# Fixing TensorE's order in the chunk recurrence of a hybrid RWKV-7 / RG-LRU block

## The chip, the cores and the metric

The kernel runs on one core of a Trainium2 chip. The metric is the device time of one execution in microseconds (us), less is better. Times of the kernel before come from three runs; the profile comes from one more execution.

## The reference, cut to what matters

One block over 512 frames of width 1024: a token mixer of two branches, then cross-attention into a memory of 256 rows, then a gated ConvFFN. The change lies in the token mixer, where one input projection of 4864 columns feeds all of it:

```python
h = rms_norm(x, norm_mix_g[l])
proj = h @ w_in[l] + b_in[l]
y_a = rwkv7_branch(proj[..., :cb0], ...) @ w_branch_a[l]
y_b = rglru_branch(proj[..., cb0:cb1], proj[..., cb1:cb2], ...) @ w_branch_b[l]
merged = sigmoid(proj[..., cb2:cg1]) * y_a + sigmoid(proj[..., cg1:]) * y_b
x = x + merged @ w_mix_out[l]
```

The first branch is a recurrence over time for 8 heads of 64:

```python
sa = einsum('bhij,bhj->bhi', state, a_t)
state = state * w_t[:, :, None, :] + sa[..., None] * b_t[:, :, None, :] + v_t[..., None] * k_t[:, :, None, :]
y_t = einsum('bhij,bhj->bhi', state, r_t)
```

The second is a convolution of width 4, two gates and a linear scan (`a = exp(log_a)`, `h_t = a_t h_{t-1} + u_t`), times `gelu(py)`.

## The kernel before

All activations lie with channels on the 128 partitions and the 512 frames along the free axis. A projection of 128 output columns (a "block") accumulates 8 steps over 1024 input rows. Each step is three TensorE products of 128x512, because every operand is split in a high and a low part (`mm3`, lines 159 to 163: high x high, high x low, low x high; lines 160 to 162 of the trace). Weights stream in units of 128x1024: SyncE loads them, ScalarE casts the high part (`win_h`), VectorE subtracts it from the original (`win_l`, line 115). The input projection has 38 blocks. Blocks 0 to 13 feed the RWKV branch, blocks 14 to 17 the convolution and the gates of the RG-LRU branch (`px_gates`), 18 to 21 its gelu (`py_block`), 22 to 37 the merge gates (`gate_block`). `IN_REST` lists the last 24 of them in the order of issue: 22 to 37, then 14 to 21. The first three are issued early.

The recurrence is worked in 8 chunks of 64 frames, with all heads at once. One chunk (`chunk`) is a chain of small TensorE groups, with the steps of other engines between them:

- `x`: the state and the chunk's values against the keys (`UV`, `AK`); VectorE copies it to `Xs`.
- `y`, first half: what the state adds to the output.
- `u`: `Xs` through the inverted chunk matrix; ScalarE copies one half to `UV`, VectorE the other.
- `vr`: the next chunk's values turned round (`rows_v`); VectorE takes their mean (`vm`) and subtracts it into the next `UV`.
- `s`: the new state; VectorE scales it (`Sn`) and writes it into the next `UV`, and prepares `SP`.
- `y`, second half; ScalarE copies it to `yT`.
- `kbr`: the next chunk's keys turned round (`rows_kb`), two halves; ScalarE copies them to `KBr`.

The accumulator banks are shared: `vr` and `kbr_0` use one (tag "kv"), `s` and `kbr_1` another ("s"), `x` and `u` a third ("xu"), `y` a fourth. A group that takes over a bank waits until the last reader of it is done.

What sets the order: the whole recurrence is emitted first, under a very high priority, and the rest of the input projection after it in the program. A scheduler then builds one fixed list for each engine. It takes by priority what it estimates to be ready, so projection products fall between the small groups wherever it thinks that one has to wait. On VectorE a part of the recurrence's steps is kept in program order (`pin`). Each engine works through its list in order on the chip, and an instruction whose operand isn't ready holds up all that stand behind it.

The RG-LRU part of the same stretch: for each of four branches `b`, `px_gates` evacuates the block (ScalarE's Identity), adds three shifted terms on VectorE (line 802), multiplies the two gate matrices (`ga`, `gx`, lines 806 and 808) on TensorE, and after each pair `px_scan` runs table functions on ScalarE and a scan into `YB` on VectorE (line 824). The tile `xb` has two buffers, so branch 2 takes over that of branch 0. `group_norm` normalizes `y`, half by half. The products `yb_ps` of the second branch follow.

At the other end of the kernel the ConvFFN's hidden blocks come in pairs (`fx_ps`, `fyz_ps`); the last pair is blocks 20 and 21. VectorE then forms their activation (`fs`, `fa`, `graw`) and the low parts of the late blocks (`gl`, `gr`). The output products `fo_ps` need `wfo_h` and `wfo_l` of the output weights and the split blocks `g`.

Of the kernel before, what the change touches and what calls it, by code (L numbers as in the profile page):

```python
# [32 lines left out]
NEARLY = 3  # L33
IN_ORDER = IN_RWKV + IN_REST
# [19 lines left out]
def hybrid_block_kernel(ctx: ExitStack, tc: tile.TileContext, xT_d, mT_d, pv_d, cst_d, win_d, wk_d, wv_d,  # L54
# [95 lines left out]
    def sum_exact(ps, blocks, src, pool, tag, name, **kw):  # L150

        hi = pool.tile(list(src.shape), F32R, tag=tag, name=f"{name}_h", **kw)
        lo = pool.tile(list(src.shape), F32R, tag=tag, name=f"{name}_l", **kw)
        S.copy(hi, src)
        V.tensor_tensor(lo, src, hi.bitcast(F32), ALU.subtract)
        PE.matmul(ps, blocks, hi, start=True, stop=False)
        PE.matmul(ps, blocks, lo, start=False, stop=True)

    def mm3(ps, lh, ll, rh, rl, start, stop, **kw):
        first = PE.matmul(ps, lh, rh, start=start, stop=False, **kw)  # L160
        PE.matmul(ps, lh, rl, start=False, stop=False, **kw)  # L161
        PE.matmul(ps, ll, rh, start=False, stop=stop, **kw)  # L162
        return first
# [407 lines left out]
    def gate_block(b):  # L571
        ps = inproj(22 + b)
# [4 lines left out]
    for jp in range(2):  # L577
# [10 lines left out]
        for j in js:  # L588
            if j == 3:
                for i in IN_REST[:NEARLY]:  # L590
                    gate_block(i - 22)
# [76 lines left out]
    pin = tc.keep_in_program_order  # L668
# [4 lines left out]
    def rows_v(c):  # L673
# [3 lines left out]
        for e in range(2):  # L677
            hs, oh = half[e], half[1 - e]
            for j in range(NPAIR):
                o = ps[oh, j * HD:(j + 1) * HD]  # L680
                src = vT[hs, j, c * HD:(c + 1) * HD]
                if e:
                    PE.transpose(o, src, ident[hs, hs])
                else:
                    PE.matmul(o, src, ident[hs, hs], start=True, stop=True)
# [8 lines left out]
    def rows_kb(c):  # L694
        KBr = ch.tile([P, 2, NPAIR, HD], F32, tag="KBr", name=f"KBr{c}", bufs=2)
        for e in range(2):
            ps = ch_ps(f"kbr{c}_{e}", ("kv", "s")[e])
            for j in range(NPAIR):
                PE.transpose(ps[:, j * HD:(j + 1) * HD], kb_cols(j, e, c), ident[half[e], half[e]])
# [6 lines left out]
    def chunk(c, UV, KBr, SP):  # L706
# [3 lines left out]
        for j in range(NPAIR):  # L710
            for e in range(2):
                PE.matmul(psx[half[e], j * HD:(j + 1) * HD], AK[:, e, j * NC + c, 0:HD], UV[:, e, j, :],
                          start=True, stop=True)
# [3 lines left out]
        for j in range(NPAIR):  # L717
            for e in range(2):
                PE.matmul(psy[half[e], j * HD:(j + 1) * HD], UV[:, e, j, :], AK[:, e, j * NC + c, HD:P],
                          start=(j == 0), stop=False)  # L720
        psu = ch_ps(f"u{c}", "xu")
        for j in range(NPAIR):
            for e in range(2):
                hs = half[e]
                PE.matmul(psu[hs, j * HD:(j + 1) * HD], BZ[hs, j * NC + c, 0:HD], Xs[hs, j, :],
                          start=True, stop=True)
        S.copy(UV[half[0], 0], j3(psu[half[0], 0:256]))
        pin(V.tensor_copy(UV[half[1], 1], j3(psu[half[1], 0:256])))
        if not last:
            nUV = rows_v(c + 1)  # L730
            pss = ch_ps(f"s{c}", "s")
            for j in range(NPAIR):
                for e in range(2):
                    PE.matmul(pss[half[e], j * HD:(j + 1) * HD], KBr[:, e, j, :], UV[:, e, j, :],
                              start=True, stop=True)
        for j in range(NPAIR):
            for e in range(2):
                hs = half[e]
                PE.matmul(psy[hs, j * HD:(j + 1) * HD], UV[hs, e, j, :], BZ[hs, j * NC + c, HD:P],
                          start=False, stop=(j == NPAIR - 1))  # L740
# [24 lines left out]
    ya2 = pa.tile([P, 2, 4, T], F32R, tag="AR", name="ya2")  # L765


    def group_norm(hf, jp, ps, psg):
# [9 lines left out]
        sum_exact(ps, bonesr, y2.rearrange("p j t -> p (j t)"), tp, "xb", f"gv{nm}", bufs=2)  # L778
# [18 lines left out]
    def px_gates(b):  # L797
        ps = inproj(14 + b)
# [6 lines left out]
        psa = rw_ps(f"ga{b}", prg, tag="rg")  # L805
        PE.matmul(psa, rg[:, 0, b, :], xb, start=True, stop=True)
        psx = rw_ps(f"gx{b}", prg, tag="rg")
        PE.matmul(psx, rg[:, 1, b, :], xb, start=True, stop=True)
        ga = tp.tile([P, T], F32, tag="ga", name=f"ga{b}", bufs=2)
        gx = tp.tile([P, T], F32, tag="gx", name=f"gx{b}", bufs=2)  # L810
        tab(ga, psa, AF.Sigmoid, bias=par("b_ga", b))
# [449 lines left out]
```

## Time and profile before

| what | value |
|---|---|
| median of 3 runs | 936.24 us (935.5 to 937.24) |
| profiled execution | 938.62 us, its span 936.8 us |
| granted TensorE clock, mean | 0.997 |
| TensorE busy | 917.8 us of the span |
| VectorE busy | 638.1 us |
| ScalarE busy | 468.9 us |
| DMA, mean rate | 183 GB/s |
| input projection products (line 160 of the trace) | 304, 404 ns mean |

Times in the trace run from the start of the span. A TensorE duration covers the pipelined flight of a product, so successive products overlap; what a product costs is read from start to start. The trace writes two records for a product of plain float32 operands, and one for the split ones and for transposes. A group's row gives line, engine, operation, output and inputs, shape, count, busy time and mean; behind the second bar stands idle time before it and what ended it. In a timeline, brackets show an idle time and its releaser.

### The profile page before, as it was taken

Reading aid. Unit: us, or ns where it says so; the run is one execution under the profiler, and the core shown is the slowest. Engines: PE = TensorE matmul, PEld = TensorE weight load, DVE = VectorE, ACT = ScalarE, POOL = GpSimd, SP = SyncE. Lnnn points to the kernel's source line nnn. Section 1 sums busy time; section 2 is a strip of 40 time slices with the busy share of each in tenths; the row PEclk is TensorE's granted clock in tenths of the full one; section 3 lists DMA queues with packets and bytes.
Section 4 is the critical chain, followed back from the end, with each engine's and each line's share of the span. In section 5 each row is a group of like instructions: output and inputs, shape, how many; then the busy total and the mean of one; then the engine's idle time right before and its main releaser. Section 6 shows DMA issues by size and latency. Waiting matters only on the chain.

```text
span 936.8 us, 14783 instructions
## 1 busy us (share of the span) xinstructions
PE 917.8 (98%) x5856; PEld 770.8 (82%) x5856; DVE 638.1 (68%) x1043; ACT 468.9 (50%) x711; POOL 87.9 (9%) x101
## 2 busy tenths in 40 slices
PE   6999999999999999999999999999999999999996
PEld 6778777788877667777887777999999999888886
DVE  7774688668845767775575578788888778833333
ACT  6565665522335276334454466766556556532221
POOL 0102211000022200001111111111111000000000
PEclk9999999999999999999999999999999999999998
DMA  8778787364599922758886668799999755422202
GB/s 273 262 255 238 174 220 190 122 170 143 158 225 194 192 35 77 218 181 221 216 226 158 167 136 195 220 264 266 259 273 252 228 188 187 140 90 90 92 22 91
DMA packets 87813, 171.16 MB, mean 183 GB/s; under 512 B 23552, under 2 KB 28800, under 8 KB 87744
## 3 DMA queue, kind: packets, MB, share of 16 engines
q1 hardware_dynamic: 61728, 111.10, 36.9%
q0 software_dynamic: 18688, 47.19, 25.0%
q10 hardware_dynamic: 7328, 11.92, 3.8%
q8 instruction: 46, 0.75, 0.3%
q14 instruction: 23, 0.19, 0.1%
HBM read 158.92 MB, written 57.41 MB: 231 GB/s over the span
## 4 chain that ended last, share of the span: by engine, by line
PE 95%; DMA 2%; ACT 1%; DVE 1%; issue 0%; POOL 0%; DVEq 0%; SPq 0%; ACTq 0%
PE in_ps L162 8%; PE in_ps L161 8%; PE in_ps L160 8%; PE fx_ps L160 4%; PE fx_ps L162 4%; PE fx_ps L161 4%; PE fo_ps L161 4%; PE fo_ps L160 4%; PE fo_ps L162 4%; PE fyz_ps L160 3%; PE fyz_ps L162 3%; PE fyz_ps L161 3%; PE co_ps L160 2%; PE mix_ps L160 2%; PE q_ps L161 2%; PE mix_ps L161 2%
## 5 line engine op out<-in xcount | busy, mean ns | idle before, releaser
L161 PE MATMUL in_ps<-hT,win_h 128*128 128x512 f32 x304 | 123.6, 407 | 0.0
L162 PE MATMUL in_ps<-hT,win_l 128*128 128x512 f32 x304 | 122.8, 405 | 0.0
L126 ACT CAST wfi_h<-wfi_r 128x1024 fp32r<-128x1024 f32 x77 | 81.0, 1052 | 83.4 <-PE fx_ps L161 28.2
L160 PE MATMUL in_ps<-hT,win_h 128*128 128x512 f32 x304 | 122.2, 404 | 0.0
L127 DVE TENSOR_TENSOR wfi_l<-wfi_r,wfi_h 128x1024 fp32r<-128x1024 f32 x77 | 94.2, 1223 | 39.0 <-ACT wfi_h L126 38.6
L420 POOL DMA_DIRECT2D dS<-in_wfi x66 | 66.6, 1036 | 458.5 <-PE in_ps L160 152.3
L114 ACT CAST win_h<-win_r 128x1024 fp32r<-128x1024 f32 x38 | 39.9, 1050 | 87.7 <-PE in_ps L161 79.2
L115 DVE TENSOR_TENSOR win_l<-win_r,win_h 128x1024 fp32r<-128x1024 f32 x38 | 46.4, 1222 | 50.2 <-ACT win_h L114 50.1
L161 PEld LDWEIGHTS in_ps<-hT,win_h 128*128 128x128 f32 x304 | 57.0, 188 | 15.7 <-issue 1.9
L160 PEld LDWEIGHTS in_ps<-hT,win_h 128*128 128x128 f32 x304 | 57.0, 188 | 15.3 <-issue 1.4
L162 PEld LDWEIGHTS in_ps<-hT,win_l 128*128 128x128 f32 x304 | 57.0, 187 | 15.1 <-issue 1.7
L115 DVE TENSOR_TENSOR wfo_l<-wfo_r,wfo_h 128x1024 fp32r<-128x1024 f32 x22 | 26.9, 1224 | 52.1 <-ACT wfo_h L114 52.1
L114 ACT CAST wfo_h<-wfo_r 128x1024 fp32r<-128x1024 f32 x22 | 23.1, 1048 | 62.1 <-PE fo_ps L161 61.4
L160 PE MATMUL fx_ps<-hq,wfi_h 128*128 128x256 f32 x176 | 50.1, 285 | 1.2 <-ACT wfi_h L126 0.9
L162 PE MATMUL fx_ps<-hr,wfi_l 128*128 128x256 f32 x176 | 49.7, 283 | 0.0
L160 PE MATMUL fx_ps<-hr,wfi_h 128*128 128x256 f32 x176 | 49.7, 282 | 0.0
L160 PE MATMUL fyz_ps<-hq,wfi_h 128*128 128x256 f32 x176 | 49.4, 281 | 0.0
L161 PE MATMUL fx_ps<-hr,wfi_h 128*128 128x256 f32 x176 | 49.4, 280 | 0.0
L161 PE MATMUL fx_ps<-hq,wfi_h 128*128 128x256 f32 x176 | 49.3, 280 | 0.0
L161 PE MATMUL fyz_ps<-hq,wfi_h 128*128 128x256 f32 x176 | 49.2, 280 | 0.0
L162 PE MATMUL fx_ps<-hq,wfi_l 128*128 128x256 f32 x176 | 49.0, 278 | 0.0
L162 PE MATMUL fyz_ps<-hq,wfi_l 128*128 128x256 f32 x176 | 49.0, 278 | 0.0
(421 smaller groups left out, 2514.2 us busy)
## 6 DMA issues: line engine op xcount, KB each, us to landing
dS<-in_wfi POOLq DMA_DIRECT2D x66, 512.0 KB, 8.3
wfi_r<-dS SPq DMA_DIRECT2D x44, 512.0 KB, 6.0
win_r<-in_win SPq DMA_DIRECT2D x38, 512.0 KB, 4.2
wfi_r<-in_wfi SPq DMA_DIRECT2D x33, 512.0 KB, 5.8
dS<-dS POOLq DMA_DIRECT2D x22, 512.0 KB, 5.5
wfo_r<-in_wfo SPq DMA_DIRECT2D x22, 512.0 KB, 3.4
wv_r<-in_wv SPq DMA_DIRECT2D x8, 512.0 KB, 5.9
dG<-gs ACTq DMA_DIRECT2D x16, 256.0 KB, 2.1
```

Source lines behind the costliest of these rows:

```text
L114: S.copy(hi[:, o:o + n], raw[:, o:o + n])
L115: V.tensor_tensor(lo[:, o:o + n], raw[:, o:o + n], hi[:, o:o + n].bitcast(F32), ALU.subtract)
L126: S.copy(hi, raw)
L127: V.tensor_tensor(lo, raw, hi.bitcast(F32), ALU.subtract)
L160: first = PE.matmul(ps, lh, rh, start=start, stop=False, **kw)
L161: PE.matmul(ps, lh, rl, start=False, stop=False, **kw)
L162: PE.matmul(ps, ll, rh, start=False, stop=stop, **kw)
L420: return lambda: nc.gpsimd.dma_start(s(out), src, **kw)
```

## The change

The order of TensorE's work through the 8 chunks is written out instead of left to the scheduler. `chunk` becomes a generator that stops after the first half of `y` and again at its end. The rest of the input projection becomes a generator too (`rest`), one step (three products) at a time. `fill(n)` takes n of its steps. 16 blocks (128 steps) come ahead of the recurrence; then each chunk gets 1 step at its first stop and 4 at its second, the last chunk only the first; what is left comes after. While `pinned` is set, `mpin` puts every product of recurrence, projection and gates in program order on TensorE. The gate products are no longer issued right after their convolution but one at a time, at every fourth step of the following blocks (`next_gate`). The first half's group norm starts ahead of blocks 20 and 21 and goes on after five steps of them. `pin` no longer fixes VectorE's program order as a whole, it chains the recurrence's steps on VectorE among themselves.

```diff
+NMID = 16
     def sum_exact(ps, blocks, src, pool, tag, name, **kw):
...
         V.tensor_tensor(lo, src, hi.bitcast(F32), ALU.subtract)
+        yield
         PE.matmul(ps, blocks, hi, start=True, stop=False)
...
+    pinned = [False]
+    def mpin(ins):
+        return tc.keep_in_program_order(ins) if pinned[0] else ins
     def mm3(ps, lh, ll, rh, rl, start, stop, **kw):
-        first = PE.matmul(ps, lh, rh, start=start, stop=False, **kw)
+        first = mpin(PE.matmul(ps, lh, rh, start=start, stop=False, **kw))
...
-    pin = tc.keep_in_program_order
+    behind = []
+    def pin(ins):
+        if behind:
+            tc.add_manual_dep(ins.ins, behind[-1].ins.name, mybir.DependencyInfo(
+                mybir.DependencyClass.NoSync, mybir.DependencyReason.DATA), reason="order of the recurrence")
+        behind.append(ins)
+        return ins
...
+        yield 1
         psu = ch_ps(f"u{c}", "xu")
...
         S.copy(yT[:, :, c * HD:(c + 1) * HD], j3(psy[:, 0:256]))
+        if not last:
+            yield 4
         return nUV, nKB, SP
...
-    with tc.high_priority(offset=1000000):
-        UV, KBr, SP = rows_v(0), rows_kb(0), None
-        for e in range(2):
-            V.memset(UV[half[e], e], 0.0)
-        for c in range(NC):
-            UV, KBr, SP = chunk(c, UV, KBr, SP)
...
+    def px_gate(b, i, xb):
+        ps = rw_ps(f"g{'ax'[i]}{b}", prg, tag="rg")
+        mpin(PE.matmul(ps, rg[:, i, b, :], xb, start=True, stop=True))
+        g = tp.tile([P, T], F32, tag=("ga", "gx")[i], name=f"g{'ax'[i]}{b}", bufs=2)
+        tab(g, ps, AF.Sigmoid, bias=par(("b_ga", "b_gx")[i], b))
+        return g
...
+    def rest():
+        pair, gates = [], []
+        def next_gate():
+            if gates:
+                b, xb, g = gates[0]
+                g.append(px_gate(b, len(g), xb))
+                if len(g) == 2:
+                    pair.append(px_gated(b, xb, *g))
+                    gates.pop(0)
+            if len(pair) == 2:
+                for p in pair:
+                    px_scan(*p)
+                pair.clear()
+        for n, i in enumerate(IN_REST[NEARLY:]):
+            if i in (20, 21):
+                norm = group_norm(0, i - 20, rw_ps(f"gv0_{i - 20}", prg, "rg"), rw_ps(f"gg0_{i - 20}", prg, "rg"))
+                next(norm)
+            ps = mm_ps(f"in_ps{i}")
+            for kb in range(KB):
+                wh, wl = uin.next()
+                ins = mm3(ps, wh, wl, h2[:, 0, kb, :], h2[:, 1, kb, :], kb == 0, kb == KB - 1)
+                if NSUM.get(i) and kb % (KB // NSUM[i]) == 0:
+                    sum_behind(ins)
+                if kb % 4 == 3:
+                    next_gate()
+                if kb == 5 and i in (20, 21):
+                    next(norm, None)
+                yield n
+            if i < 18:
+                gates.append((i - 14, px_conv(i - 14, ps), []))
...
+    fill(KB * NMID)
+    pinned[0] = True
+    with tc.high_priority(offset=1000000):
+        state = rows_v(0), rows_kb(0), None
...
+    for c in range(NC):
+        steps = chunk(c, *state)
+        try:
+            while True:
+                with tc.high_priority(offset=1000000):
+                    n = next(steps)
+                fill(n)
+        except StopIteration as end:
+            state = end.value
+    pinned[0] = False
+    fill(None)
```

How this moves instructions is seen at three places. Counts in these rows are instructions; numbers in names are buffers.

The first place is TensorE at the start of chunk 0. Before, from the first `vr` on:

```order
L685 MATMUL vr_1928<-cst,vT 64x64 x4
L683 MATMUL vr_1928<-cst,vT 64x64 x4
L699 MATMUL kbr_1_1948<-cst,KBt 128x64 x4
L160 MATMUL in_ps_3183<-hT_0_87,win_h_3186 128x512
L161 MATMUL in_ps_3183<-hT_1_88,win_h_3186 128x512
L162 MATMUL in_ps_3183<-hT_0_87,win_l_3187 128x512
L160 MATMUL in_ps_3183<-hT_0_87,win_h_3186 128x512
L712 MATMUL x_1956<-UV_1927,AK 64x64
L719 MATMUL y_1967<-AK,UV_1927 64x64
L161 MATMUL in_ps_3183<-hT_1_88,win_h_3186 128x512
L699 MATMUL kbr_0_1942<-cst,KBt 128x64 x4
L712 MATMUL x_1956<-UV_1927,AK 64x64 x7
```

The same place after the change, also from the first `vr` on:

```order
L700 MATMUL vr_2519<-cst,vT 64x64 x4
L698 MATMUL vr_2519<-cst,vT 64x64 x4
L714 MATMUL kbr_0_2533<-cst,KBt 128x64 x4
L714 MATMUL kbr_1_2539<-cst,KBt 128x64 x4
L727 MATMUL x_2547<-UV_2518,AK 64x64 x8
L734 MATMUL y_2558<-AK,UV_2518 64x64 x8
L168 MATMUL in_ps_2573<-hT_0_87,win_h_2576 128x512
L169 MATMUL in_ps_2573<-hT_1_88,win_h_2576 128x512
L170 MATMUL in_ps_2573<-hT_0_87,win_l_2577 128x512
L741 MATMUL u_2584<-Xs_2556,BZ 64x64 x8
```

Both halves of `kbr` now follow `vr` directly, and `x` and `y` are whole; a run of three projection products comes before `u`.

The second place is the first gate product within the recurrence, `ga` of branch 2 (`xb_3166` before, `xb_2567` after). On TensorE before, in chunk 3:

```order
L162 MATMUL in_ps_3329<-hT_0_87,win_l_3333 128x512
L160 MATMUL in_ps_3329<-hT_0_87,win_h_3332 128x512
L725 MATMUL u_2225<-Xs_2214,BZ 64x64 x8
L806 MATMUL ga_3172<-xb_3166,rg 128x512
L734 MATMUL s_2250<-UV_2153,KBr_2184 64x64
L739 MATMUL y_2216<-BZ,UV_2153 64x64
```

On TensorE after the change, the last products of chunk 0's run of 12 and the start of chunk 1:

```order
L170 MATMUL in_ps_2573<-hT_0_87,win_l_2577 128x512
L819 MATMUL ga_2657<-xb_2567,rg 128x512
L168 MATMUL in_ps_2573<-hT_0_87,win_h_2576 128x512
L169 MATMUL in_ps_2573<-hT_1_88,win_h_2576 128x512
L170 MATMUL in_ps_2573<-hT_0_87,win_l_2577 128x512
L727 MATMUL x_2666<-UV_2595,AK 64x64 x8
L734 MATMUL y_2677<-AK,UV_2595 64x64 x8
```

The gate moved from chunk 3 to the end of chunk 0, ahead of chunk 1's `x`. On VectorE after the change, what stands from chunk 0's `Sn` on to the first step of that branch's convolution:

```order
L760 TENSOR_TENSOR Sn_2639<-s_2609,PC 128x256
L833 SCALAR_TENSOR_TENSOR gx_2448<-ga_2430,gx_2448 128x512
L766 COPY UV_2595<-Sn_2639 64x256 x2
L771 TENSOR_TENSOR SP_2643<-UV_2595,PC 64x256 x2
L834 MEMSET gx_2448 128x1
L835 TENSOR_TENSOR xb_2401<-xb_2401,gx_2448 128x512
L833 SCALAR_TENSOR_TENSOR gx_2499<-ga_2481,gx_2499 128x512
L836 SCALAR_TENSOR_TENSOR YB<-ga_2430,xb_2401 128x512
L834 MEMSET gx_2499 128x1
L835 TENSOR_TENSOR xb_2452<-xb_2452,gx_2499 128x512
L836 SCALAR_TENSOR_TENSOR YB<-ga_2481,xb_2452 128x512
L812 SCALAR_TENSOR_TENSOR xb_2567<-in_ps_2458,pv,xb_2567 128x511
```

The whole scan of branches 0 and 1 stands ahead of the convolution here, with no step of chunk 1 between. Before, steps of chunks 1 and 2 stood between these rows.

The third place is far from the edit: the start of the ConvFFN's output products. On TensorE before:

```order
L160 MATMUL fo_ps_8048<-g_0_5485,wfo_h_8051 128x512
L161 MATMUL fo_ps_8048<-g_0_5485,wfo_h_8051 128x512
L162 MATMUL fo_ps_8048<-g_0_5485,wfo_l_8052 128x512
L160 MATMUL fo_ps_8048<-g_1_5498,wfo_h_8051 128x512
L161 MATMUL fo_ps_8048<-g_1_5498,wfo_h_8051 128x512
```

On TensorE after the change:

```order
L168 MATMUL fo_ps_8050<-g_0_5487,wfo_h_8053 128x512
L169 MATMUL fo_ps_8050<-g_0_5487,wfo_h_8053 128x512
L168 MATMUL fo_ps_8140<-g_0_5487,wfo_h_8113 128x512
L169 MATMUL fo_ps_8140<-g_0_5487,wfo_h_8113 128x512
L170 MATMUL fo_ps_8050<-g_0_5487,wfo_l_8054 128x512
```

On VectorE before, around the first `wfo_l`:

```order
L1140 TENSOR_TENSOR gl_8013<-graw_7016,gl_8013 128x512
L115 TENSOR_TENSOR wfo_l_8052<-wfo_r_8049,wfo_h_8051 128x1024
L1113 TENSOR_TENSOR fs_7990<-fyz_ps_7766,sn_7768 128x512
L1113 TENSOR_TENSOR fs_8001<-fyz_ps_7767,sn_7769 128x512
L1114 TENSOR_TENSOR fs_7990<-fs_7990,rf 128x512
```

And after the change, where 18 rows that begin with `fs` of block 20 come first:

```order
L1200 TENSOR_TENSOR gr_8018<-graw_8000,gr_8018 128x512
L1185 SCALAR_TENSOR_TENSOR graw_8011<-fx_ps_7767,fa_8006 128x256
L1186 SCALAR_TENSOR_TENSOR graw_8011<-p_21_7773,fa_8006 128x256
L116 TENSOR_TENSOR wfo_l_8054<-wfo_r_8051,wfo_h_8053 128x1024
L1200 TENSOR_TENSOR gr_8018<-graw_8011,gr_8018 128x512
```

The first `wfo_l` moved from ahead of blocks 20 and 21 to behind them, and `fo_ps` starts two output blocks before it asks for a low part.

More of the change, by code (lines that the diff above doesn't have):

```diff
@@ L733, in chunk @@
                 for e in range(2):
-                    PE.matmul(pss[half[e], j * HD:(j + 1) * HD], KBr[:, e, j, :], UV[:, e, j, :],
-                              start=True, stop=True)
+                    mpin(PE.matmul(pss[half[e], j * HD:(j + 1) * HD], KBr[:, e, j, :], UV[:, e, j, :],
+                                   start=True, stop=True))
         for j in range(NPAIR):
```

76 lines of the change are left out of this document (33 added, 43 removed).

## The prediction

> **What bounds the kernel now.** I read the page first: the busy shares, then the chain of work that ended last.
>
> ```profile
> PE 917.8 (98%) x5856; PEld 770.8 (82%) x5856; DVE 638.1 (68%) x1043; ACT 468.9 (50%) x711; POOL 87.9 (9%) x101
> PE 95%; DMA 2%; ACT 1%; DVE 1%; issue 0%; POOL 0%; DVEq 0%; SPq 0%; ACTq 0%
> ```
>
> TensorE (PE) is never free for long, and 95% of the closing chain is its own work. So time can be saved only by making its stream shorter, and every new wait on it is paid in full. The change touches the stretch from the first `vr` product (286.4 us) to the first `yb_ps` product (371.1 us). The table by windows, cut at chunk boundaries, sums up that stretch:
>
> ```profile
> sum 84.70, PE 84.68 PEld 60.48 DVE 60.58 ACT 46.72 POOL 10.50; mean PE 10.59 PEld 7.56 DVE 7.57 ACT 5.84 POOL 1.31
> ```
>
> PE is busy for 84.68 of 84.70 us, VectorE (DVE) for 60.58. No wait is left to remove; what can be removed is the price of alternating. The timeline of PE in chunk 0 and chunk 1 (start, duration, line, count):
>
> ```profile
> 293.26 0.50 PE L162 MATMUL in_ps<-hT,win_l 128*128 128x512 f32 x1
> 293.68 0.68 PE L725 MATMUL u<-Xs,BZ 64*64 64x64 f32 x14
> 294.29 0.50 PE L160 MATMUL in_ps<-hT,win_h 128*128 128x512 f32 x1
> ...
> 295.88 0.33 PE L734 MATMUL s<-UV,KBr 128*64 128x64 f32 x2
> ```
>
> and where `s` and `y` are cut:
>
> ```profile
> 305.74 0.33 PE L734 MATMUL s<-UV,KBr 128*64 128x64 f32 x2
> 306.00 0.32 PE L739 MATMUL y<-BZ,UV 64*64 64x64 f32 x2
> 306.25 0.50 PE L160 MATMUL in_ps<-hT,win_h 128*128 128x512 f32 x1
> ```
>
> A lone projection product between small ones holds PE from 293.26 to 293.68, 0.42 us. Six in a row hold it from 294.29 to 295.88, 1.59 us, 0.265 each. From the two equations, one more product in a run costs 0.234 us and each run about 0.19 on top; I use 0.20. Two `s` records alone cost 0.26, two `y` 0.25. Now chunk 4, where the recurrence happens to stand together:
>
> ```profile
> 328.39 0.48 PE L699 MATMUL kbr<-cst,KBt 64*128 64x64 f32 x8
> 328.79 0.69 PE L712 MATMUL x<-UV,AK 128*64 128x64 f32 x16
> 329.31 0.64 PE L719 MATMUL y<-AK,UV 128*64 128x64 f32 x16
> 329.88 0.67 PE L685 MATMUL vr<-cst,vT 64*64 64x64 f32 x8
> 330.48 0.41 PE L683 MATMUL vr<-cst,vT 64*64 64x64 f32 x4
> 330.82 1.13 PE L806 MATMUL ga<-xb,rg 128*128 128x512 f32 x2
> ```
>
> and a little later:
>
> ```profile
> 333.78 0.69 PE L734 MATMUL s<-UV,KBr 128*64 128x64 f32 x16
> 334.39 0.68 PE L739 MATMUL y<-BZ,UV 64*64 64x64 f32 x16
> 335.01 0.49 PE L160 MATMUL in_ps<-hT,win_h 128*128 128x512 f32 x1
> ```
>
> Start to start: `kbr` 0.40 us, `x` 0.52, `y` 0.57, `vr` 0.94, `u` 0.61 (by the like-sized `s`), `s` 0.61, `y` again 0.62: 4.27 per chunk, on PE alone.
>
> **The change, part by part.** It adds no work: the same 120 projection products stand in the stretch.
>
> *Grouping.* Counted in the two orders, 45 runs of large products become 22: 23 x 0.20 = 4.6 us. In six chunks `s` and `y` are no longer cut in 1 + 7 products: the four pieces cost 0.26 + 0.25 + 2 x 0.61 (by the 0.61 of a near-full group of 14, 293.68 to 294.29) = 1.73 against 1.23, so 6 x 0.5 = 3.0. Five split `kbr` pairs, by the same rows some 0.3 each, 1.5. **Gain 9 us** (7 to 11).
>
> *First `kbr`.* It takes over the bank of `vr` and so waits for VectorE's mean and two subtractions of `vr`. Before, `kbr_1` and four projection products cover that; now `kbr_0` comes directly behind `vr`. Three steps of 256 columns, by the like-sized `SP` below 0.42 each, and two hand-overs: about 1.45 us of waiting. **+1.4** (1 to 2).
>
> *First gate.* This is the largest new term. The product `ga` of block 16 stands in chunk 3 before, after `u`; now it stands 9 projection products into chunk 0's run of 12, and PE may not pass it. Its operand `xb2` needs the buffer of `xb0` (two buffers), free when VectorE has scanned `YB` for branch 0; then ScalarE's Identity and VectorE's convolution. The groups on VectorE between 286 and 372 us:
>
> ```profile
> L824 DVE TENSOR_TENSOR_SCAN YB<-ga,xb 128x512 f32<-128x512 f32 x4 | 4.9, 1215 | 0.0
> L823 DVE TENSOR_TENSOR xb<-xb,gx 128x512 f32<-128x512 f32 x4 | 2.8, 688 | 0.0
> L821 DVE SCALAR_TENSOR_TENSOR gx<-ga,gx 128x512 f32<-128x512 f32 x4 | 2.7, 687 | 1.2 <-ACT gx L235 1.1
> L755 DVE TENSOR_TENSOR SP<-UV,PC 64x256 f32<-64x256 f32 x12 | 5.0, 420 | 0.4
> L802 DVE SCALAR_TENSOR_TENSOR xb<-in_ps,pv,xb 128x511 f32<-128x511 f32 x2 | 1.4, 746 | 0.0
> L750 DVE COPY UV<-Sn 64x256 f32<-64x256 f32 x2 | 1.1, 549 | 0.0
> ```
>
> ScalarE in chunk 0 (line 235 holds the table functions):
>
> ```profile
> 290.31 0.73 ACT L235 ACTIVATE ga<-ga,dp 128x512 f32<-128x512 f32 x1
> 290.94 0.71 ACT L235 ACTIVATE gx<-gx,eps 128x512 f32<-128x512 f32 x1
> 294.40 0.37 ACT L727 COPY UV<-u 64x256 f32<-64x256 f32 x1 [2.75 <-PE u L725]
> 294.67 0.63 ACT L235 ACTIVATE gx<-gx 128x512 f32<-128x512 f32 x1
> ```
>
> Count from the start of `vr0`. PE: 0.94 + 1.45 wait + 0.40 + 0.52 + 0.57 + 3 products 0.90 + `u` 0.61 = 5.4; + 0.94 + 0.61 + 0.62 + 0.40 + 9 products 2.3 = **10.2 us**, where it reaches `ga`. The other side: in the new order ScalarE copies `u` ahead of the three table steps of branch 0, so from 5.4 run 0.37 + 0.63 + 0.63 + 0.63, and `gx` is ready at 7.7. VectorE then has, in its fixed queue: `gx` 0.69, two copies 1.10, two `SP` 0.84, `xb` 0.69, `gx` of branch 1 0.69, scan 1.22, `xb` 0.69, scan 1.22, three convolution steps 3 x 0.74 and small ones 0.3. That is 9.6 us, 9.0 where neighbours overlap. `xb2` is ready at **16.8**. PE waits **6.6 us** (4 to 9). Before, the recurrence items were interleaved with this work while PE had projection products to run.
>
> *Other chunks.* Behind `u` PE has only `vr`, 0.94, against ScalarE's copy 0.37, VectorE's 0.42 and three hand-overs; so `s` waits nothing to 0.5 us where VectorE is otherwise busy, `kbr` likewise. Seven times 0.3: **+2** (0 to 4).
>
> *Tail.* Four steps, 12 products or 2.9 us, are left behind chunk 7. They must hide the copy of `y`, its square, the split and the sum of two groups for the second half, and the table loads, while VectorE is behind. Bounds 0 (hidden, as now) and 6 (none); I take the middle, and one more for `yb_ps`: **+4**.
>
> *Side effect at the end of the ConvFFN.* The changed list also comes out differently near 800 us. VectorE forms `wfo_l0` only after both last FFN blocks, and PE has four products of high halves, two of `fo_ps0` and two of `fo_ps1`, before it needs `wfo_l0`. The rows of before, there:
>
> ```profile
> 798.17 1.23 DVE L115 TENSOR_TENSOR wfo_l<-wfo_r,wfo_h 128x1024 fp32r<-128x1024 f32 x1
> 799.32 1.28 DVE L1113 TENSOR_TENSOR fs<-fyz_ps,sn 128x512 f32<-128x512 f32 x2
> ```
>
> The last subtractions on VectorE, and the first product of the output on PE:
>
> ```profile
> 811.02 1.29 DVE L1140 TENSOR_TENSOR gr<-graw,gr 128x512 fp32r<-128x512 f32 x2
> 802.56 0.41 PE L160 MATMUL fo_ps<-g,wfo_h 128*128 128x512 f32 x1
> ```
>
> From `fs` at 799.32 to 811.02 are 11.7 us with three more `wfo_l` (1.15 each, start to start) among them. Now those three leave, three more subtractions of 0.64 come ahead: 11.7 - 3.5 + 1.9 = 10.1. With `wfo_l` out of the way `fs` can begin near 798.3; `wfo_l0` ends near 798.3 + 10.1 + 1.2 = 809.6. PE is there at 802.56 + 4 x 0.234 = 803.5. **+6** (0, if the queue is not that late, to 8).
>
> *A cold clock.* At the start of the kernel, PE after its only long wait:
>
> ```profile
> 7.04 0.58 PE L160 MATMUL k_ps<-m,wk_h 128*128 128x256 f32 x1 [7.04 <-ACT m L281]
> ```
>
> a little behind it, and from 13 us on:
>
> ```profile
> 8.27 0.41 PE L162 MATMUL k_ps<-m,wk_l 128*128 128x256 f32 x1
> 8.48 0.41 PE L160 MATMUL k_ps<-m,wk_h 128*128 128x256 f32 x1
> ```
>
> and from 13 us on:
>
> ```profile
> 13.03 0.29 PE L160 MATMUL k_ps<-m,wk_h 128*128 128x256 f32 x1
> 13.15 0.28 PE L161 MATMUL k_ps<-m,wk_h 128*128 128x256 f32 x1
> ```
>
> After 7.04 us without work a product starts each 0.21 us; from 13.03 on each 0.12. Over some 4.5 us that loses 4.5 x (1 - 0.12/0.21) = 1.9, call it 2 us. Two waits of 6 to 7 us are new: **+4** (0 to 5). [...]
>
> *Moved without a price.* The first half's group norm now starts with blocks 20 and 21 instead of before 19, and `px_gates` is cut in three; both stay under projection products of PE, and what peeps out is in the tail's bounds. The DMA issues of SyncE and GpSimd stand in the same order in both kernels, and DMA has 2% of the chain; a later load costs nothing here.
>
> Sum: -9 + 1.4 + 6.6 + 2 + 4 + 6 + 4 = **+15.0 us**. The profiled run took 938.62 us with a span of 936.8, 1.8 around it; so 953.6 for a run like it. The median of the runs is 936.24, 2.4 lower; the forecast in its terms is **951 us**.
>
> **Rivals.** *Only one of the long waits is real.* Against the gate: VectorE was busy only part of that time.
>
> ```profile
> 290.00:300.00 10.00, 10.00 (x109) 6.97 (x109) 4.08 (x10) 5.61 (x11) 2.31 (x3) 1.00 0.99 271
> ```
>
> 4.08 of 10 us, so there is slack, if the table steps come early. Without that wait and its cold clock: 951 - 8.6 = 942. Without the seam at 800 us: 951 - 8 = 943. Together 21%.
>
> *The other side.* The grouping wins. The point that decides is the arrival of `xb2` at 10.2 us after `vr0` or before; it takes that ScalarE's copy of `u` isn't what holds the table steps, so that VectorE's 9 us run in the 5.9 us that it stood idle there. The seam must be covered too. Then -9 + 1.4 + 2 + 1 = -4.6: 932 us. For it speaks the 4.08 above; against it that ScalarE's last step on `gx` ran at 294.67, directly behind the copy of `u`, and PE then had nothing that depended on it. 6%.
>
> *A draw.* Gate covered, seam exposed without a cold clock, tail hidden: 936 us. 5%.
>
> *More waits.* The backlog on VectorE is handed on from chunk to chunk and each `s` and `kbr` waits a microsecond more: 7 x 1 = 7, 958 us. 10%. That grouping doesn't happen at all can be excluded; the order is fixed.
>
> **How the numbers follow.** Forecast 58%, 951 us. The range takes in the one-wait cases (942) and the backlog (958), with 2 to 3 us on each for the term of grouping: 939 to 961. About 0.2%, 2 us, is what a measurement of this kernel can tell from no change. Faster 6%, within it 5%, slower 89%.
>
> **What would show it.** Runs of 12 and 3 in PE's timeline, no lone `in_ps`, and a chunk without waits near 4.3 + 4.6 us, show the gain. A wait of PE at the first `ga` of about 6.6 us that ends with VectorE, 16.8 us after `vr0`, shows the gate. A wait of `fo_ps` for `wfo_l` of about 6 us shows the seam. Spacing of 0.4 rather than 0.23 us behind them shows the clock. The prediction is wrong if PE waits less than 3 us in either place, or if `yb_ps` starts before 371 us.

## The result, and the profile after

The changed kernel takes **961.93 us** (median of 6 runs, 959.25 to 968.28) against 936.19 us before (6 runs, 935.1 to 937.24): ratio 1.0279, 95% interval 1.025 to 1.0308. It is slower by 25.7 us; the forecast was 951 with a range up to 961, so the sign was right and the time 0.9 us outside the range. The profiled execution is the longest of the six, 968.28 us with a span of 966.5 and a mean granted clock of 0.978; the others have 0.985 to 0.987. Of two later kernels (the ones with a third stop) one execution each was disturbed, of the first the profiled one, and the comparisons and readings leave it out.

Busy shares and the chain that ended last, after:

```profile
PE 925.9 (96%) x5856; PEld 778.2 (81%) x5856; DVE 637.4 (66%) x1043; ACT 471.8 (49%) x713; POOL 87.8 (9%) x101
PE 85%; DVE 6%; DMA 3%; ACT 3%; issue 1%; SPq 0%; DVEq 0%; ACTq 0%
```

The instruction counts are those of before but for two on ScalarE. PE's own share of the chain fell from 95% to 85%, and VectorE, DMA and ScalarE took what it lost: PE now waits. For whom, the waits of PE say (who waits, its line, on whom; us in total, times, the longest):

```profile
PE fo_ps L170 <- DVE wfo_l L116: 5.0, 1, 5.0
PE ga L819 <- DVE xb L814: 4.5, 1, 4.5
PE prT_ps L1041 <- DVE ex L1039: 4.0, 1, 4.0
PE kbr L714 <- DVE UV L705: 3.7, 4, 1.5
PE yb_ps L168 <- DVE mB L930: 1.5, 1, 1.5
PE gv L158 <- ACT gv_h L155: 1.3, 2, 0.9
PE fo_ps L168 <- ACT wfo_h L115: 1.1, 1, 1.1
```

`ga`, `kbr` and `fo_ps` were forecast. `prT_ps` was not: it stands in the cross-attention, at 502 us, where the recurrence has long ended.

Cut at the first product of each stage, the two profiled executions differ so (us, from starts read to 0.1 us; the parts add up to the difference of the spans, 29.7):

| from | to | before | after | difference |
|---|---|---|---|---|
| start | `vr` | 286.4 | 285.7 | -0.7 |
| `vr` | `yb_ps` (the recurrence) | 84.7 | 98.3 | +13.6 |
| `yb_ps` | `ya_ps` | 23.4 | 24.8 | +1.4 |
| `ya_ps` | `q_ps` | 67.4 | 68.0 | +0.6 |
| `q_ps` | `co_ps` (the attention) | 67.4 | 74.0 | +6.6 |
| `co_ps` | `fo_ps` | 273.3 | 272.7 | -0.6 |
| `fo_ps` | end | 134.2 | 143.0 | +8.8 |

More than half of the loss in these two executions is not in the recurrence. Within it, PE's timeline shows the first wait, and what follows it:

```profile
288.20 0.47 PE L714 MATMUL kbr<-cst,KBt 64*128 64x64 f32 x8 [1.49 <-DVE UV L705]
288.60 0.69 PE L727 MATMUL x<-UV,AK 128*64 128x64 f32 x16
289.12 0.64 PE L734 MATMUL y<-AK,UV 128*64 128x64 f32 x16
289.68 0.79 PE L168 MATMUL in_ps<-hT,win_h 128*128 128x512 f32 x1
290.27 0.63 PE L169 MATMUL in_ps<-hT,win_h 128*128 128x512 f32 x1
290.70 0.63 PE L170 MATMUL in_ps<-hT,win_l 128*128 128x512 f32 x1
```

From 290.27 on a projection product starts every 0.43 us instead of every 0.234: the clock is halved, after a wait of only 1.49 us. The table by windows of 4 us (busy time and count of PE, PE's weight load, DVE, ACT and POOL; granted clock; DMA share; GB/s) gives it in numbers:

```profile
284.00:288.00 4.00, 2.70 (x18) 1.54 (x17) 2.19 (x7) 1.73 (x2) 0.60 (x1) 1.00 0.98 206
288.00:292.00 4.00, 3.80 (x59) 2.95 (x62) 2.12 (x4) 2.65 (x4) 0.71 (x1) 0.71 0.98 229
292.00:296.00 4.00, 4.00 (x60) 3.44 (x55) 2.88 (x8) 2.66 (x6) 0.00 (x0) 0.50 1.00 326
296.00:300.00 4.00, 4.00 (x13) 2.81 (x9) 3.40 (x7) 3.64 (x6) 2.29 (x2) 0.51 0.42 60
300.00:304.00 4.00, 0.18 (x1) 0.00 (x0) 3.85 (x7) 0.78 (x1) 0.00 (x0) 0.91 0.99 153
```

PE is busy for all of 292 to 300 us and runs at half speed (granted clock 0.50 and 0.51); then it stands still for the gate, while VectorE works 3.85 of 4 us.

### The profile page after: what moved, and what is told of

Same layout as the page of the kernel before. It is cut to its first block, busy times and chain, and to the rows that moved or that the text cites. A ratio compares the mean times of both kernels' runs of the same rounds, so it can differ in the third digit from the quotient of the medians.

```text
span 966.5 us, 14772 instructions
## 1 busy us (share of the span) xinstructions
PE 925.9 (96%) x5856; PEld 778.2 (81%) x5856; DVE 637.4 (66%) x1043; ACT 471.8 (49%) x713; POOL 87.8 (9%) x101
## 4 chain that ended last, share of the span: by engine, by line
PE 85%; DVE 6%; DMA 3%; ACT 3%; issue 1%; SPq 0%; DVEq 0%; ACTq 0%
PE in_ps L168 8%; PE in_ps L169 7%; PE in_ps L170 7%; PE fx_ps L168 4%; PE fx_ps L170 4%; PE fx_ps L169 4%; PE fo_ps L170 4%; PE fo_ps L168 4%; PE fo_ps L169 4%; PE fyz_ps L168 3%; PE fyz_ps L170 3%; PE fyz_ps L169 3%; PE co_ps L169 2%; PE co_ps L168 2%; PE co_ps L170 2%; PE sc L569 1%
## 5 line engine op out<-in xcount | busy, mean ns | idle before, releaser
L168 PE MATMUL in_ps<-hT,win_h 128*128 128x512 f32 x304 | 127.4, 421 | 0.0
L169 PE MATMUL in_ps<-hT,win_h 128*128 128x512 f32 x304 | 124.4, 410 | 0.0
L168 PEld LDWEIGHTS in_ps<-hT,win_h 128*128 128x128 f32 x304 | 58.2, 192 | 17.1 <-issue 2.4
L169 PEld LDWEIGHTS in_ps<-hT,win_h 128*128 128x128 f32 x304 | 58.4, 192 | 16.2 <-issue 3.2
```

The source lines that it names most:

```text
L168: first = mpin(PE.matmul(ps, lh, rh, start=start, stop=False, **kw))
L169: mpin(PE.matmul(ps, lh, rl, start=False, stop=False, **kw))
```

## The experiments

Each is an edit of the changed kernel. Ratios are to the kernel before, on the same chip; 0.001 is 0.94 us. The theory tested has three parts: waits in the recurrence (who sets them), the halved clock (what starts it), and two losses far away (output stage and attention).

### What grouping is worth when nobody waits

The recurrence's products and the gate products of blocks 16 and 17 read tiles that are long there, and VectorE and ScalarE read such a tile in place of the products' results. It leaves the results out, not the work. No product of the recurrence then waits for an operand, or for an accumulator bank that still has to be read. An example of each kind:

```diff
-AK[:, e, j * NC + c, 0:HD], UV[:, e, j, :],
+AK[:, e, j * NC + c, 0:HD], AK[:, 1 - e, j, 0:HD],
-pin(V.tensor_copy(Xs, j3(psx[:, 0:256])))
+pin(V.tensor_copy(Xs, AK[:, 0, 0:NPAIR, 0:HD]))
-mpin(PE.matmul(ps, rg[:, i, b, :], xb, start=True, stop=True))
+mpin(PE.matmul(ps, rg[:, i, b, :], xb if b < 2 else gup, start=True, stop=True))
```

> Leaves out: in the recurrence TensorE's products, and the gate products of blocks 16 and 17, read tiles that are ready long before, and VectorE and ScalarE read such a tile in place of those products' results; the instructions, their sizes and TensorE's order are those of the changed kernel. So TensorE waits for no one in the recurrence, and the length of the stretch from the first vr to the first yb_ps product, beside the 84.8 us of before, is what grouping is worth by itself. As in the prediction (9 us): 75.8. As the rows of the all-repairs kernel say, less its waits (6 to 8 us): 77 to 79. If runs of equal products are worth little (under 4 us): 81 or more. With the attention's and the seam's losses (6.6 and 8.7) still in, the time would be 936 - 7 + 15 = 944 us, 942 to 945; 948 or more if grouping is worth under 4. If the low clock follows waits, the stretch has none; if it follows runs of small products alone, the clock falls near 280 to 290 us here too.

Ratio 1.0099 (1.0061 to 1.0137), 947.03 us, 2 us over the expected range. The stretch takes 82.4 us (284.2 to 366.6), and it still holds waits, one of them made by the edit itself (`gup` lands late). The longer ones in PE's timeline:

```profile
296.07 2.05 PE L819 MATMUL ga<-gup,rg 128*128 128x512 f32 x2 [3.22 <-DMA gup<-in_gup]
324.55 0.47 PE L168 MATMUL in_ps<-hT,win_h 128*128 128x512 f32 x1 [2.12 <-DVE xb L812]
366.10 0.50 PE L158 MATMUL gv<-gv_h,bonesr 128*128 128x512 f32 x1 [0.97 <-ACT gv_h L155]
```

With 0.7 more for `gv` and 0.8 for `gg` that is 7.8 us, and the halved clock behind `ga` costs 1.6 (the pair and the three products behind it take 3.18 us, from 296.07 to 299.25; a like group elsewhere in this run 1.56). So 82.4 - 7.8 - 1.6 = 73.0 us are PE's own: grouping alone is worth **11.7 us**, more than any of the three expectations. It is the difference of two profiled executions, less waits read from one of them, so an estimate to about 1 us. Waits hidden inside groups don't swell it: in the stretch of before, no small product starts more than 0.16 us behind another. A chunk of the run without dependences, and behind it the same stretch in the changed kernel:

```profile
330.73 0.69 PE L750 MATMUL s<-AK 128*64 128x64 f32 x16
331.34 0.68 PE L755 MATMUL y<-BZ,AK 64*64 64x64 f32 x16
331.96 0.47 PE L714 MATMUL kbr<-cst,KBt 64*128 64x64 f32 x8
332.36 0.50 PE L168 MATMUL in_ps<-hT,win_h 128*128 128x512 f32 x1
```

```profile
321.60 1.05 PE L750 MATMUL s<-UV,KBr 128*64 128x64 f32 x16
322.58 0.68 PE L755 MATMUL y<-BZ,UV 64*64 64x64 f32 x16
323.45 0.70 PE L714 MATMUL kbr<-cst,KBt 64*128 64x64 f32 x8 [0.19 <-DVE UV L705]
324.08 0.50 PE L168 MATMUL in_ps<-hT,win_h 128*128 128x512 f32 x1
```

From `s` to the first projection product: 1.63 us without dependences, 2.48 with them, and only 0.19 of the 0.85 between is shown as idle. The rest hides in groups that start and then pause: `s` lasts 0.98 start to start instead of 0.61, with its operand late, and the two halves of `kbr` run one behind the other, 0.63 instead of 0.40, with the second half's bank not yet free. Chunks 1, 2 and 6 pay 0.81 to 0.85. Taken for all seven that have an `s`, this is 6 us, most of it in no row of the waits; it is an estimate, since in the others the halved clock or the group norm's products come between.

### The waits of the recurrence

Two of the 128 projection steps between `vr0` and `kbr0`, to cover the first wait:

```diff
-    fill(KB * NMID)
+    fill(KB * NMID - 2)
...
-        state = rows_v(0), rows_kb(0), None
+        UV0 = rows_v(0)
...
+    fill(2)
+        state = UV0, rows_kb(0), None
```

> The changed kernel with two of the 128 steps ahead of the recurrence moved between the first vr and the first kbr. Theory A: the first kbr no longer waits, the clock stays at 1.00 until the first gate; what is gained there is waited for at the gate, which then waits some 8 us, since VectorE is no earlier; cold behind it; 957 to 962 in all. [...]

Ratio 1.0259 (1.023 to 1.0288), 962.11 us: nothing gained. The wait of `kbr` in chunk 0 is gone and the gate's is 4.7 us; the clock falls all the same, and earlier (below).

The gates of blocks 16 and 17 a whole block (8 steps) later:

```diff
-                if kb % 4 == 3:
+                if kb % 4 == 3 and i != 17:
```

> The changed kernel with the four gate products of branches 2 and 3 one block later (from chunk 2 on). Theory A: no wait at a gate, 4.5 us less, and no cold stretch behind it, 2.5 us less, but chunk 0 still cold from its first kbr on: about 955. [...] Theory C (VectorE is the bound of the stretch, waits move elsewhere): 960 or more, with the same waiting at kbr or s.

Ratio 1.0256 (1.023 to 1.0282), 961.2 us. The `ga` wait is gone; in its place stand these:

```profile
PE gv L158 <- ACT gv_h L155: 4.3, 3, 3.0
PE kbr L714 <- DVE UV L705: 3.5, 5, 1.5
PE s L750 <- DVE UV L744: 1.5, 3, 0.9
```

The group norm, which queues behind the gates on ScalarE and VectorE, is late in its turn (`gv` 4.3 us instead of 1.3).

Both edits together:

> Both edits of the two runs before together. Theory A: clock 1.00 from 285 us to the end of chunk 3, recurrence stretch some 12 us shorter than in the changed kernel, 948 to 950 in all. Theory C: waits move to kbr and s, 957 or more.

Ratio 1.0275 (1.0249 to 1.0301), 962.7 us. No better than the changed kernel itself.

The gates later by only half a block (4 steps):

```diff
-                if kb % 4 == 3:
+                if kb % 4 == 3 and (i, kb) != (17, 3):
```

> The changed kernel with the gates of branches 2 and 3 four steps later (half of what was tried before), so that the first comes in chunk 1, some 19 us behind the first vr, when its operand is ready by the profile (19.5 us). If the gate's wait can be saved without making the tail late: 4 to 5 us less, about 957. If VectorE and ScalarE bind the stretch as a whole, the wait moves to gv again: 961.

Ratio 1.0238 (1.0222 to 1.0253), 957.73 us: 3.8 us of the 26 back. No `ga` wait, `gv` at 1.3 us as in the changed kernel, the stretch 90.3 us. Of the three places tried, the middle one is the best; it doesn't make the chain of VectorE and ScalarE shorter.

### The halved clock

The wait of 1.49 us does not always bring the clock down. The profiles of four experiments that leave the start of chunk 0 alone show the same wait. In three (gates late, gates half late, seam) the clock is at 0.50 behind it for 3.4 us, in the changed kernel for 10.2 us, and in the fourth (keys, further down) it stays at 1.00:

```profile
280.00:298.70 18.70, 13.37 (x174) 9.84 (x174) 12.18 (x26) 11.99 (x19) 4.88 (x5) 1.00 0.82 181
```

So what that wait costs differs from one execution to the next, and a kernel's one profile doesn't tell its usual price.

Idle products put into the waits: 6 of 128x512 between `vr0` and `kbr0`, 18 into the gate's own bank ahead of `ga` of block 16. They add no result, only work.

```diff
+        for _ in range(6):
+            mpin(PE.matmul(dps, bonesr, h2[:, 0, 0, :], start=True, stop=True))
...
+        if b == 2 and i == 0:
+            for _ in range(18):
+                mpin(PE.matmul(ps, bonesr, h2[:, 0, 0, :], start=True, stop=True))
```

> The changed kernel with products that compute nothing put where TensorE waits in chunk 0: 6 of 128x512 between the first vr and the first kbr, 18 ahead of the first gate, into banks that are overwritten. What TensorE waits for comes no earlier. Theory A (after a stretch of small products with a short wait, TensorE's clock is halved, and this is the larger part of the loss; busy it stays up): the granted clock is 1.00 through chunk 0 and 1, 7 us less than the changed kernel, about 955. Theory B (only the waits themselves cost): 962, no change.

Ratio 1.0236 (1.0213 to 1.026), 958.84 us, and a stretch of 92.1 us instead of 98.3. Its windows, the same eight us as above:

```profile
292.00:296.00 4.00, 4.00 (x23) 3.32 (x24) 3.84 (x10) 3.95 (x7) 1.66 (x2) 1.00 0.66 181
296.00:300.00 4.00, 3.13 (x14) 2.24 (x12) 3.88 (x6) 0.81 (x2) 0.64 (x1) 1.00 0.98 145
```

The clock stays at 1.00 through the whole recurrence. Work that is good for nothing makes the kernel some 4 us faster here; the interval of the ratio just touches that of the changed kernel, and the stretch is the clearer sign.

The same with small products, of 64x64, 9 and 40 of them:

```diff
-            mpin(PE.matmul(dps, bonesr, h2[:, 0, 0, :], start=True, stop=True))
+            mpin(PE.matmul(dps[64:128, 0:64], vT[0:64, 0, 0:64], ident[0:64, 0:64], start=True, stop=True))
```

> As the first run (TensorE is kept busy where it waits in chunk 0), but with small idle products: 9 of 64x64 ahead of the first kbr, 40 ahead of the first gate, about as long. Theory A1 (the clock follows how much of the array works, and small products are too little): granted clock 0.5 in chunk 0 and behind the gate though TensorE has no idle there, 961 to 965. Theory A2 (the clock follows idle time of TensorE): 1.00 as with the large ones, 959.

Ratio 1.0247 (1.0228 to 1.0265), 960.04 us; the stretch is 92.1 us again, and the clock 1.00 from 280 to 308 us (the time itself can't be told from the changed kernel's). So products of 64x64 in the waits keep the clock as well as large ones do, in the one profile of each; that the recurrence's small products pull it down by themselves is not borne out. The run without dependences says the same: its clock is 1.00 from 280 to 295.7 us, and falls only at the end of the wait of 3.22 us at `ga`.

But filling waits isn't all. In the kernel with both edits (the first wait covered, the gates late) the clock falls at 280.3 us, ahead of `vr0`. The 3.4 us before that, the 6.8 us at half clock, and the timeline there:

```profile
276.90:280.30 3.40, 3.35 (x83) 2.80 (x83) 0.69 (x1) 1.26 (x2) 1.46 (x2) 1.00 0.62 111
280.30:287.10 6.80, 6.80 (x42) 4.74 (x39) 2.92 (x7) 1.04 (x1) 2.02 (x3) 0.50 1.05 203
```

```profile
279.34 0.40 PE L170 MATMUL in_ps<-hT,win_l 128*128 128x512 f32 x1
279.80 1.59 PE L653 MATMUL zo<-ZA,Hs 32*32 32x32 f32 x32
281.31 1.11 PE L700 MATMUL vr<-cst,vT 64*64 64x64 f32 x8
282.92 0.79 PE L168 MATMUL in_ps<-hT,win_h 128*128 128x512 f32 x1
```

PE is busy for 3.35 of the 3.40 us ahead of the fall. In them stand groups of 16 products of 32x32 (`zh`, `zo`; 32 records each, since the trace writes two for a product) and two large products; the edit took two steps from between them and `vr`. The kernel that only covers `kbr0` shows it in the same place (0.72 and 0.50 from 280 to 288 us). In the changed kernel and in the one before it the same groups ran at full clock (1.00 from 276 to 288 us), with two more projection steps between. In these two profiles a row of mostly 32x32 products, with PE busy for 3.35 of 3.40 us in the one shown, thus goes with a fall to 0.50 as a wait of 1.49 us does in others; what decides it was not measured.

### The output stage and the attention

The first unit of `wfo` is taken up ahead of the last FFN pair's sums on VectorE, and `fo_ps0` and `fo_ps1` keep the written order:

```diff
-    uf = Units(wfo_d, "wfo")
...
+        if m0 + NQ >= FB:
+            uf = Units(wfo_d, "wfo")
+            uf.fill()
...
+                tc.add_manual_dep(ins.ins, lows[-1].ins.name, mybir.DependencyInfo(
...
+        pinned[0] = m < 2
```

> The changed kernel with the order at the ConvFFN's output as it was before: VectorE forms the first wfo_l ahead of the last two blocks, and TensorE keeps fo_ps in program order. If the two waits there (5.0 and 1.1 us) and the cold stretch behind them (2.5 us) cost what the profile shows: 8.5 us less, about 953. If the time until fo_ps is bound by VectorE in sum, whatever the order: less than 3 us.

Ratio 1.0214 (1.0198 to 1.0229), 955.65 us: 6 us back. From `fo_ps` to the end 136.2 us instead of 143.0; the wait is 1.8 us instead of 5.0 + 1.1, and the clock is 1.00 in every window between 820 and 840 us.

In the attention PE's `prT_ps` waits for the softmax, and that stands in VectorE's and ScalarE's queues behind the second half of the keys. The rows of ScalarE and VectorE in the changed kernel:

```profile
498.35 1.05 ACT L1007 CAST K<-kvK 128x1024 fp32r<-128x1024 f32 x1 [4.63 <-DMA kvK<-dK]
499.43 1.22 DVE L1008 TENSOR_TENSOR K<-kvK,K 128x1024 fp32r<-128x1024 f32 x1 [4.43 <-ACT K L1007]
502.70 0.69 PE L1041 MATMUL prT_ps<-cst,ex 128*128 128x128 f32 x2 [3.99 <-DVE ex L1039]
```

ScalarE waits 4.63 us for the keys. Their load, by the tile's own view (first and last issue), after and before:

```profile
L1003 ACTq DMA_DIRECT2D kvK<-dK x2: 377/380/383, 480.4 to 490.6; - x2
```

```profile
L943 ACTq DMA_DIRECT2D kvK<-dK x2: 377/380/383, 465.4 to 473.9; - x2
```

Counted from the first `q_ps` product (476.8 and 461.9), the first half is issued at 3.6 and 3.5 us, the second at 13.8 and 12.0: ScalarE issues it itself, behind casts that come 1.8 us later. And it takes 7.7 us to land instead of 4.3:

```profile
kvK<-dK ACTq DMA_DIRECT2D x1, 512.0 KB, 7.7
```

```profile
kvK<-dK ACTq DMA_DIRECT2D x1, 512.0 KB, 4.3
```

The test leaves the load where it is and puts the cast and split of that half behind the softmax of head 0, which doesn't need it:

```diff
-    for i, what in ((0, "K"), (0, "V"), (1, "V"), (1, "K")):
+    for i, what in ((0, "K"), (0, "V"), (1, "V")):
...
+        if hd == 0:
+            load_kv(1, "K")
```

> The changed kernel with the cast and the split of the second half of the memory's keys put behind the softmax of the first attention head on ScalarE and VectorE (the load is issued as before). If the late load, standing ahead of the softmax in both queues, makes TensorE's wait at prT (4.0 us) and the cold stretch behind it: 4 to 6 us less, about 956, and no wait at prT over 1 us. If the load is late only by chance in the profiled run: no change, 962.

Ratio 1.0228 (1.021 to 1.0247), 957.64 us: some 5 us back. The `prT_ps` wait is gone and the attention takes 67.3 us, as before the change (67.4). The stage takes 71.4 to 74.1 us in all eight experiments above and below that leave it as it is, so the lateness is not the chance of one execution. That the queue behind the keys makes it is shown. Why the load took 3.4 us longer was not tried apart; two GpSimd loads start beside it in the changed kernel (490.32 and 493.90 us), one before the change (475.13).

### All repairs, and a third stop

The gates half a block late, 6 idle products at `kbr0`, the seam and the keys together:

> The repairs together: gates half late, 6 idle products of 128x512 at the first kbr, and the two order repairs of attention and ConvFFN. If the losses add up: 962 - 8.5 - 5 - 5 = 943, still over the kernel before, since the stretch of the recurrence is then 88 to 90 us against 84.8. If grouping gains what its saved switches say (9 us): 936 or less.

Ratio **1.0113** (1.0091 to 1.0136), 944.98 us: about 16 of the 25.7 us are back, and it is still slower than before. The stretch takes 88.7 us at a clock of 0.995 for the whole run. Its waits there:

```profile
PE kbr L715 <- DVE UV L706: 2.3, 3, 1.3
PE s L751 <- ACT UV L744: 1.3, 2, 1.1
PE gv L159 <- ACT gv_h L156: 1.3, 2, 0.9
PE s L751 <- DVE UV L745: 1.1, 2, 0.8
```

To cover `s` too, a third stop of one step between `vr` and `s`, and 3 instead of 4 steps later:

```diff
             nUV = rows_v(c + 1)
+            yield 1
...
-            yield 4
+            yield 3
```

> All repairs, and a third stop in each chunk, between vr and s: 1, 1 and 3 steps instead of 1 and 4. The step there covers the wait of s for the copies of u, some 0.4 to 1.1 us in each of 7 chunks, for 0.2 us of one more switch: 945 - 2 to 4 = 941 to 943; no cold stretch in the recurrence, since no run of small products is longer than 3 us. If switching is the larger price: 946.

Ratio 1.0104 (1.0085 to 1.0123): no better than without it. That the clock holds where no run of small products is longer than 3 us was the author's estimate, and no run shows such a bound; the mean clock of this kernel's executions is 0.989 to 0.991, that of the all-repairs kernel's 0.992 to 0.995. With two real steps in place of the idle products:

> As the run before, but with two steps of real work between the first vr and the first kbr in place of the idle products: 1.5 us less, 940, if the clock holds; if the 32x32 products ahead of the first vr, now with fewer large ones among them, halve the clock there as in the fourth run (280 to 288 us): 943 or more.

Ratio 1.0115 (1.0088 to 1.0141). The waits for `s` fall to 0.5 us, as meant, but the gate's is back:

```profile
PE ga L821 <- DVE xb L816: 4.3, 1, 4.3
PE kbr L715 <- DVE UV L706: 2.3, 2, 1.3
PE s L752 <- ACT UV L744: 0.5, 2, 0.3
```

The stretch takes 93.6 us, and the clock is low from 283.0 to 286.4 us, as feared, and again behind the gate. Each order that relieves one wait hands it to another; none of these orders beats the one before, in which the recurrence's items lie between projection products and PE is busy for 84.68 of 84.70 us.

## Why the prediction was right in sign and short in size

The sum of +15 fell short by 14.7 us in the profiled execution and by 10.9 in the medians. The step that failed in kind is "Moved without a price": it put the keys' load at nothing without a row for it, and the attention lost 6.6 us. Two more steps were right in kind and far too small, "Other chunks" (+2, measured +7.9) and "A cold clock" (+2 for the wait in the recurrence, +9.4 left over for it). Two errors the other way, in grouping and at the gate, hid 4.8 us of this; that is luck.

The terms, in the profiled execution (the last column adds up to the 29.7 us between the spans):

| the prediction's part | forecast | measured | from |
|---|---|---|---|
| Grouping | -9 | -11.7 | stretch without dependences |
| First `kbr` | +1.4 | +1.5 | row at 288.20 |
| First gate | +6.6 | +4.5 | waits |
| Other chunks | +2 | +7.9 | 7 x 0.85, and 1.9 in longer `kbr` and `s` waits |
| Tail | +4 | +3.4 | `gv` and `gg` 2.0, `yb_ps` stage 1.4 |
| Side effect at the end of the ConvFFN, with its cold clock | +8 | +8.8 | stage |
| A cold clock, the other wait | +2 | +9.4 | what is left of the stretch's +13.6 |
| Moved without a price: attention | 0 | +6.6 | stage |
| the rest | 0 | -0.7 | stages |

The profiled execution lies 6.3 us above its median, the one of before 2.4; so 3.9 of the 29.7 are not in the median, which leaves 25.8, the result. Executions at a mean clock of 0.987 instead of 0.978 are those 6 us shorter. If the 3.9 come off the clock's term, about 5.5 us of it are typical; this is an estimate.

**Grouping** was right in kind and too small. The prediction's sign for it, "a chunk without waits near 4.3 + 4.6 us", was too high: a chunk without waits or gates takes 7.83 us (`x` to `x`, 327.51 to 335.34 in the run without dependences), 3.95 for its small products and 3.88 for its 15 projection products. By the prediction's own prices these 15 are 3.9, so the 4.6 was a slip, and no term of the sum uses it. Its 4.27 for the small products counts `u` and `vr` one behind the other, 0.61 + 0.94; in the new order they interleave and take 1.24. Seven times 0.31 is 2.2 us, most of the 2.7 that the term lacked, as an estimate.

**First `kbr`** is as forecast. **First gate** too: 6.2 and 6.3 us in the two experiments where the clock had not fallen as far ahead of it (keys and seam); 4.5 in the profiled run, because PE at half speed comes late to it. The match has some luck in it: in the run with the keys behind the head the operand comes 17.7 us after `vr0` and PE 11.5 us after it, for forecasts of 16.8 and 10.2, and the two errors nearly cancel.

**Other chunks** failed in size. "`s` waits nothing to 0.5 us ... seven times 0.3" looked for a wait between groups; the real one lies mostly inside them, 0.85 us a chunk. The rival "more waits", 7 us and 958 us at 10%, had the better number, though not its backlog handed on from chunk to chunk: chunks 1 and 6 pay the same.

**Side effect at the end of the ConvFFN** is confirmed by undoing it: the wait came as 5.0 + 1.1 us for a forecast of 6, and the stage as 8.8 for 8 with its cold clock.

**A cold clock** failed in its condition: the step took a wait of 6 to 7 us to be needed, and counted two. In the recurrence one of 1.49 us sufficed, though not in every execution, and in the three experiments with real steps between `vr0` and `kbr0` the clock fell to 0.50 with no wait ahead of it. The row that gave the price is a spacing, 0.21 and then 0.12 us; the clock in the trace of the kernel before reads 1.00 there (7 to 13 us), so that a lowered clock made that spacing was the author's estimate. Idle products in the waits kept it at 1.00 from 280 to 308 us, so it does hang on what PE does there; they made the stretch 6.2 us shorter (98.3 to 92.1). With the 1.7 us that the halved clock hid of the gate's wait (6.2 less 4.5) this accounts for 7.9 of the 9.4; the rest is a remainder that no run explains.

**Moved without a price** is the step that was wrong in kind. It looked at the DMA issues of SyncE and GpSimd only, and from DMA's 2% of the chain concluded that "a later load costs nothing here". The keys' load is issued by ScalarE, whose order moved; it came 1.8 us later and took 3.4 longer, and the softmax queues behind it. Undone, it gives some 5 us back and the kernel takes 957.64 us, inside the range; so does undoing the seam or the gate's place, but these had a price in the sum. A share of the chain says how often a resource ends last now; it says nothing about how much room is left.

## What to carry to other kernels

Giving TensorE long runs of equal products saves what the alternation costs (11.7 us here), but the mixture was also the cover for VectorE and ScalarE; before grouping, count for each hand-over how much independent work is left behind it. When an order list changes, look at every engine's DMA issues and at what queues behind the loads, hundreds of us further on too. And leave the dependences out once, in an experiment: the difference between that run and the real one is what all waits cost, those inside groups and the lowered clock included, once the waits that the experiment itself makes are taken off.

## What the runs showed of the hardware

The granted clock was not lost through long waits alone. It went to 0.50 behind a wait of 1.49 us, though not in every execution, and to 0.50 behind 3.40 us in which PE was busy for 3.35, with groups of 32x32 products. In the profile of the changed kernel it was low for 10.2 us (289.7 to 299.9) and four times for 6.8: from 303.3, 501.3 and 829.0, inside the waits of 4.5, 4.0 and 5.0 us, and from 344.3, at the end of one of 1.27. From 962.1 on, where PE has no more work, it was low once more. Elsewhere it was low also for 3.4 us (283.0 to 286.4 in the last kernel with a third stop). Filling the waits with products of 128x512 or of 64x64 kept it at 1.00 from 280 to 308 us, in one profile of each. Over a whole execution of the changed kernel its mean was 0.978 in one and 0.985 to 0.987 in the other five. What decides whether a wait of 1.49 us brings it down, or how long it then stays low, no run showed.

A group of matmuls that had started and then waited for an operand showed as busy, not as idle: `s` of 8 products (16 records) took 0.98 us start to start with its operand late, 0.61 without. PE's busy time rose from 917.8 to 925.9 us though its instructions are the same; such pauses and the halved clock both have a part in that.
